# Four of six w_down groups as seven block products, with x kept in memory meanwhile

## The chip, the cores and the metric

The kernel runs on one core of one Trainium2 chip. The metric is the device time of the execution in microseconds (us); the time before is the median of three runs. PE is the tensor engine, DVE the vector engine, ACT the scalar engine, POOL the general engine and SP the engine that issues the DMAs. "Row" in a fence of the instruction order is one instruction as the program lists it for its engine; such a row has no time.

## The reference, cut

A decoder trunk of two layers, float32: a retention layer, a projection of shared keys and values, a dilated-attention layer, each followed by the channel mixer that the change touches. D_MODEL is 1024, SEQ 512, D_FF 2816 (22 tiles of 128).

```
def conv_ffn(h, w_up, conv_w, conv_b, w_down):
    u = h @ w_up                                   # 512 x 5632
    gate, val = u[..., :D_FF], u[..., D_FF:]
    gp = jnp.pad(gate, ((0, 0), (CONV_WIDTH - 1, 0), (0, 0)))
    conv = conv_b
    for i in range(CONV_WIDTH):
        conv = conv + conv_w[i] * gp[:, i:i + S]
    return (jax.nn.gelu(conv, approximate=True) * val) @ w_down
...
f = conv_ffn(rmsnorm(x, norm_ffn_pre[layer]), ...)
x = x + rmsnorm(f, norm_ffn_post[layer])
```

## The kernel before, in words

**Products in two parts.** Each float32 operand is split into a high part (a cast to fp32r, on ACT) and a low part (operand less high part, on DVE). `mm3` (L208 to L210) forms a product as three matmuls: high by high, high by low, low by high. Weights come as units of 128 x 1024 floats: a DMA of 512 KB on SP's queue into a `raw` tile, the cast `whi` (L168, ACT), the low part `wlo` (L169, DVE). Tiles come from pools with a fixed number of buffers (5 each for `whi` and `wlo`), so a cast waits until PE has read the unit that held its buffer. Activations go through `split` (L198 the cast on ACT, L199 the low part on DVE).

**The FFN.** It works on transposed activations. `up(f)` takes two units of `w_up` (gate and value) against the normed h, 8 steps deep: 2 x 8 x 3 = 48 matmuls of 128 x 512 into two accumulators of PSUM (`pm`, tag "mm", 4 buffers). `gated` then makes tile f of the activations: conv on ACT (L553) and DVE (L556, twice), gelu (L559), the product with the value (L561), and the split into `ah` and `al` (8 buffers each).

`contract` multiplies a group of activation tiles by their rows of `w_down`: for each of 4 row blocks b of 128 tokens and 2 column halves c of 512, one PSUM block `po` (tag "po", 2 buffers) of 4 tiles x 3 = 12 matmuls, which `accumulate` adds to the float32 sum `m[b][:, half(c)]` in SBUF (L271 on DVE; for the first group L269, a copy on ACT). The groups are tiles 0 and 1, then 2 to 5, 6 to 9, 10 to 13, 14 to 17, 18 to 21. `up_first` computes tiles 0 and 1; then the ups of a group come, and after them the contraction of the group before it. The last group goes to `finish`, which also does the closing norm, adds to x (L305), and starts the next layer's norm (L254 or L256) and transposes (L264).

**Order.** A tile scheduler places the instructions of each engine in one queue, not always in the order in which they are written; at run time every engine works its queue in order and waits at its head. All weight loads are issued by SP, in order too. In the first FFN of the profiled execution the first matmul of the ups is at 423 us, in the second at 1359 us, and the second FFN runs to the end.

Of the kernel before, what the change touches and what calls it, by code (L numbers as in the profile page):

```python
# [10 lines left out]
F32 = mybir.dt.float32  # L11
F32R = mybir.dt.float32r
# [5 lines left out]
P = 128  # L18
# [57 lines left out]
def _run(gen):  # L76
    for _ in gen:
        pass


def _take(gen, n):
    for _ in range(n):
        next(gen)
# [13 lines left out]
def trunk(ctx: ExitStack, tc: tile.TileContext, a, out):  # L97
# [4 lines left out]
    norm = ctx.enter_context(tc.tile_pool(name="norm", bufs=1))  # L102
    small = ctx.enter_context(tc.tile_pool(name="small", bufs=5))
    ps = ctx.enter_context(tc.tile_pool(name="ps", bufs=2, space=PSUM))

# [159 lines left out]
    def accumulate(src, dst, first):  # L267
        if first:
            nc.scalar.copy(out=dst, in_=src)  # L269
        else:  # L270
            nc.vector.tensor_add(out=dst, in0=src, in1=dst)  # L271

    def contract(left, w, first, tag="po", after=None):


        for b in range(NB):
            for c in range(2):
                po = ps.tile([P, 512], F32, name="po", tag=tag, bufs=4 if tag == "mm" else 2)
                for j in range(len(w)):
                    mm3(po, left(j, b), (w[j][0][:, half(c)], w[j][1][:, half(c)]), j == 0, j == len(w) - 1)  # L280
                    if j < len(w) - 1:
                        yield
                accumulate(po, m[b][:, half(c)], first)
                if after is not None:
                    after(b, c)
                yield

    E = mybir.EngineType
    F4=1
# [251 lines left out]
    def ffn(l, pool, post, then, late, ahead=()):  # L541
        w_up, w_down = a["ffn_w_up"][l], a["ffn_w_down"][l]
        cw = lambda i, f: cols[l][:, i * FT + f : i * FT + f + 1]
        with pool as tmp:

            def up_mm(pm, w, s):
                for k in range(KT):
                    c = slice(k * P, (k + 1) * P)
                    mm3(pm[:, s], (w[0][:, c], w[1][:, c]), (hi[:, k, s], lo[:, k, s]), k == 0, k == KT - 1)

            def gated(f, pg, pv):
                t = tmp.tile([P, SEQ], F32, name="conv", tag="conv", bufs=2)
                nc.scalar.activation(t, pg, AF.Identity, bias=cw(3, f), scale=cw(2, f))  # L553
                for i in (1, 0):
                    d = 2 - i
                    nc.vector.scalar_tensor_tensor(  # L556
                        out=t[:, d:], in0=pg[:, : SEQ - d], scalar=cw(i, f), in1=t[:, d:], op0=ALU.mult, op1=ALU.add
                    )
                nc.scalar.activation(t, t, AF.Gelu_apprx_tanh)  # L559
                act = tmp.tile([P, SEQ], F32, name="act", tag="act", bufs=2)  # L560
                nc.vector.tensor_mul(out=act, in0=t, in1=pv)  # L561
                ah = tmp.tile([P, SEQ], F32R, name="ah", tag="ah", bufs=8)
                al = tmp.tile([P, SEQ], F32R, name="al", tag="al", bufs=8)
                split(act, ah, al)
                return ah, al

            def up(f):
                w = cols_unit(w_up, f * P), cols_unit(w_up, FF + f * P)
                pm = [ps.tile([P, 512], F32, name="pm", tag="mm", bufs=4) for _ in range(2)]
                for g in range(2):  # L570
                    up_mm(pm[g], w[g], slice(0, SEQ))
                return gated(f, *pm)

            def up_first(units, late):

                pm = [ps.tile([P, 512], F32, name="pm", tag="mm", bufs=4) for _ in range(4)]
                with tc.manual_schedule(engines=ORD):
                    for i in range(4):
                        if i == 3:
                            late[1]()  # L580
                        up_mm(pm[i], units[i], slice(0, SEQ // 2))
                        if i == 0:
                            late[0]()
                for i in range(4):
                    up_mm(pm[i], units[i], slice(SEQ // 2, SEQ))
                return [gated(f, pm[2 * f], pm[2 * f + 1]) for f in range(2)]

            def down(fs, act, pool=None):
                w = [unit(w_down[f * P : (f + 1) * P, :], pool=pool if i < 3 else None) for i, f in enumerate(fs)]
                return lambda j, b: [t[:, blk(b)] for t in act[j]], w  # L590

            bounds = [0, *range(2, FT + 1, 4)]
            prev = None
            for n, (f0, f1) in enumerate(zip(bounds, bounds[1:])):
                act = up_first(*late) if n == 0 else [up(f) for f in range(f0, f1)]
                if prev is not None:
                    _run(contract(*down(*prev), n == 1))
                prev = (range(f0, f1), act)
            l, w = down(*prev, tmp)
            return finish(l, w, post, then, ahead, early=tmp)  # L600

# [413 lines left out]
```

## Time and profile before

| | |
|---|---|
| median of three runs | 1729.71 us (1728.86 to 1730.98) |
| profiled execution | 1732.5 us |
| its span | 1730.7 us |
| mean granted clock of PE | 0.995 |
| PE, DVE, ACT, POOL busy | 1703.0, 934.5, 612.1, 396.8 us |
| moved by DMA | 156.10 MB |

The span is what the instructions cover; the execution's own time has 1.8 us more around it. Busy rows name line, engine, operation and "out<-in" by the program's names, then the shape, how many, the busy time, the mean of one in ns, and behind the second bar the idle time ahead of them and what ended it. In a timeline a row gives start and duration in us, and in brackets the idle time ahead and its releaser. In rows of windows each engine's busy time is followed by the number of its instructions, then the granted clock (PEclk, 1.00 is full), the DMA share and GB/s.

### The profile page before, as it was taken

The page shows a single profiled execution, that of the slowest core. Times are in us where ns is not written, and L with a number is a line of the kernel's source. Part 1 is how long each engine was busy: PE and PEld are TensorE (multiplying, and loading weights), DVE is VectorE, ACT ScalarE, POOL GpSimd, SP SyncE. Part 2 cuts the span into 40 slices and gives each one's busy share as a digit, 9 for nine tenths or more (in the row PEclk, how much of TensorE's full clock was granted, in tenths as well). Part 3 has the DMA queues.
Part 4 walks back from the last instruction along what each step waited for, and adds up shares of the span by engine and source line. Part 5 has one row for each costly group of instructions (what it writes and reads, how often), then busy time and mean ns, then how long its engine had stood idle before and what let it go on. Part 6 is the DMA issues. An engine that isn't in the chain of part 4 may idle for free.

```text
span 1730.7 us, 21655 instructions
## 1 busy us (share of the span) xinstructions
PE 1703.0 (98%) x8590; PEld 1412.4 (82%) x8590; DVE 934.5 (54%) x1470; ACT 612.1 (35%) x1070; POOL 396.8 (23%) x281
## 2 busy tenths in 40 slices
PE   9999999999999999998999999999999999999998
PEld 6888888887888888888788888888887888888886
DVE  4563545558544544558556466456474854454454
ACT  5232422325442322324144243244255534233241
POOL 1000000004000000036756656566431300000003
PEclk9999999999999999999999999999999999999999
DMA  6422322213432332331322222222221333333331
GB/s 209 130 67 86 91 97 80 86 49 98 127 97 82 110 98 85 110 109 60 96 74 74 86 74 74 79 76 78 74 74 49 94 106 97 91 102 97 89 107 49
DMA packets 202162, 156.10 MB, mean 90 GB/s; under 512 B 4989, under 2 KB 182093, under 8 KB 202062
## 3 DMA queue, kind: packets, MB, share of 16 engines
q1 hardware_dynamic: 202062, 154.73, 29.2%
q8 instruction: 67, 1.10, 0.3%
q14 instruction: 33, 0.27, 0.0%
HBM read 152.62 MB, written 2.10 MB: 89 GB/s over the span
## 4 chain that ended last, share of the span: by engine, by line
PE 91%; POOL 3%; DVE 3%; DMA 1%; issue 1%; ACT 1%; POOLq 0%; SPq 0%; DVEq 0%; ACTq 0%
PE pm L208 21%; PE pm L210 21%; PE pm L209 21%; PE po L208 6%; PE po L209 6%; PE po L210 6%; PE sc L756 2%; PE po L866 2%; PE pt L846 2%; DVE x L305 1%; PE s L450 1%; POOL r_rms L215 1%; POOL h L323 1%; DVE wlo L169 1%; PE pt L264 1%
## 5 line engine op out<-in xcount | busy, mean ns | idle before, releaser
L208 PE MATMUL pm<-hT_hi,whi 128*128 128x512 f32 (+1 forms) x1424 | 545.0, 383 | 0.0
L209 PE MATMUL pm<-hT_lo,whi 128*128 128x512 f32 (+1 forms) x1424 | 538.4, 378 | 0.8 <-DVE hT_lo L199 0.8
L210 PE MATMUL pm<-hT_hi,wlo 128*128 128x512 f32 (+1 forms) x1424 | 538.9, 378 | 0.0
L169 DVE TENSOR_TENSOR wlo<-raw,whi 128x1024 fp32r<-128x1024 f32 x275 | 371.5, 1356 | 297.0 <-ACT whi L168 293.5
L168 ACT CAST whi<-raw 128x1024 fp32r<-128x1024 f32 x275 | 286.0, 1050 | 641.0 <-PE pm L209 348.9
L208 PEld LDWEIGHTS pm<-hT_hi,whi 128*128 128x128 f32 x1424 | 268.4, 189 | 51.1 <-issue 3.2
L210 PEld LDWEIGHTS pm<-hT_hi,wlo 128*128 128x128 f32 x1424 | 268.2, 188 | 50.3
L209 PEld LDWEIGHTS pm<-hT_lo,whi 128*128 128x128 f32 x1424 | 268.6, 189 | 48.7 <-DVE hT_lo L199 1.7
L158 POOL TENSOR_TENSOR raw<-raw,cols 128x1024 f32<-128x1024 f32 x72 | 145.1, 2017 | 455.2 <-DMA raw<-in_att_w_kv 373.2
L271 DVE TENSOR_TENSOR m<-po,m 128x512 f32<-128x512 f32 x112 | 77.1, 688 | 138.0 <-PE po L210 137.8
L208 PE MATMUL pm<-whi,hT_hi 128*128 128x512 f32 (+1 forms) x384 | 142.1, 370 | 0.0
L208 PE MATMUL po<-whi,ah 128*128 128x512 f32 x352 | 137.1, 390 | 0.0
L209 PE MATMUL po<-wlo,ah 128*128 128x512 f32 x352 | 137.0, 389 | 0.0
L210 PE MATMUL po<-whi,al 128*128 128x512 f32 x352 | 136.9, 389 | 0.0
L210 PE MATMUL pm<-whi,hT_lo 128*128 128x512 f32 (+1 forms) x384 | 136.9, 356 | 0.0
L209 PE MATMUL pm<-wlo,hT_hi 128*128 128x512 f32 (+1 forms) x384 | 136.8, 356 | 0.0
L323 POOL TENSOR_TENSOR h<-m,gain 128x512 f32<-128x512 f32 x28 | 41.9, 1496 | 405.5 <-DVE m L271 405.2
L215 POOL TENSOR_TENSOR r_gn<-v_gn,nhalf 128x1 f32<-128x1 f32 x16 | 8.8, 548 | 357.4 <-DVE v_gn L480 357.4
L208 PEld LDWEIGHTS pm<-whi,hT_hi 128*128 128x128 f32 x384 | 73.0, 190 | 11.6 <-issue 1.0
L209 PEld LDWEIGHTS pm<-wlo,hT_hi 128*128 128x128 f32 x384 | 73.0, 190 | 10.9 <-DVE wlo L169 0.7
L210 PEld LDWEIGHTS pm<-whi,hT_lo 128*128 128x128 f32 x384 | 72.9, 190 | 10.6 <-DVE hT_lo L199 0.2
L208 PEld LDWEIGHTS po<-whi,ah 128*128 128x128 f32 x352 | 66.1, 188 | 14.0 <-DVE m L271 0.4
(137 smaller groups left out, 1958.5 us busy)
## 6 DMA issues: line engine op xcount, KB each, us to landing
raw<-in_ffn_w_up SPq DMA_DIRECT2D x88, 512.0 KB, 3.8
raw<-in_att_w_kv SPq DMA_DIRECT2D x48, 512.0 KB, 4.0
raw<-in_ret_w_in SPq DMA_DIRECT2D x47, 512.0 KB, 3.8
raw<-in_ffn_w_down SPq DMA_DIRECT2D x44, 512.0 KB, 3.2
raw<-in_att_w_q SPq DMA_DIRECT2D x24, 512.0 KB, 3.7
raw<-in_ret_w_out SPq DMA_DIRECT2D x16, 512.0 KB, 3.2
raw<-in_att_w_o SPq DMA_DIRECT2D x8, 512.0 KB, 3.2
x<-in_x SPq DMA_DIRECT2D x3, 512.0 KB, 6.8
```

The costliest lines, as they stand in the source:

```text
L158: nc.gpsimd.tensor_mul(out=dst, in0=dst, in1=gain.unsqueeze(2).broadcast_to(list(src.shape)))
L168: nc.scalar.copy(out=hi, in_=raw)
L169: nc.vector.tensor_sub(out=lo, in0=raw, in1=hi.bitcast(F32))
L208: nc.tensor.matmul(o, lhsT=l[0], rhs=r[0], start=start, stop=False)
L209: nc.tensor.matmul(o, lhsT=l[0], rhs=r[1], start=False, stop=False)
L210: nc.tensor.matmul(o, lhsT=l[1], rhs=r[0], start=False, stop=stop)
L215: behind.append(nc.gpsimd.tensor_tensor(out=r, in0=v, in1=nhalf, op=ALU.pow).ins)
L271: nc.vector.tensor_add(out=dst, in0=src, in1=dst)
L323: eng.tensor_mul(out=mg[b][c], in0=m[b][:, half(c)], in1=gain[:, half(c)])
L756: nc.tensor.matmul(pm[h][:, i, c], lhsT=q, rhs=k, start=True, stop=True)
L846: nc.tensor.transpose(out=pt[:, h, n, :], in_=p[:, h, :], identity=ident)
L866: nc.tensor.matmul(dst, lhsT=v, rhs=p, start=i == 0 and g == 0, stop=i == 7)
```

## The change

For the groups 2 to 5, 6 to 9, 10 to 13 and 14 to 17 of both layers, the product of activations (512 tokens by 512 deep) with rows of `w_down` (512 deep by 1024 columns) is formed by Strassen's scheme, in the variant with shared sums. Tokens are halved (0 to 255, 256 to 511), depth is halved into even and odd tiles of the group, columns into 0 to 511 and 512 to 1023.

- `sums` makes, for each pair of tiles, four sums of activation blocks of 256 columns and splits them: one takes the place of the second half of the even tile's `ah` and `al`, three go to new tiles `sx` (in three buffers of the tag "xwlo").
- `contract7` loads the four weight blocks (128 x 2 x 512 each, in the tags "xraw" and "xwhi"), makes four differences of weights on DVE (L303, L304, L307, L310), splits seven weight operands (`parts`, L170 and L171), and runs the seven products in the order 1, 7, 6, 4, 5, 2, 3. Each has two blocks of 128 tokens (tag "po" with 2 buffers for the first, "mm" with 4 for the second) of 2 x 3 = 6 matmuls, added to the sum of that product over the groups, `q[i]`.
- `q[i]` takes 14 blocks of 128 x 512: eight lie in `m`, six in three tiles that take x's buffers. So x goes to memory (`away`) ahead of the ups and is read back after the combination.
- `combine7` makes the four blocks of the result out of the seven sums, with 14 additions of 128 x 512 (L332), once per layer after the group 14 to 17.
- The order of work becomes: `up_first`, the writes of x, ups 2 to 6, group 2 to 5, ups 7 to 10, group 6 to 9, ups 11 to 14, group 10 to 13, ups 15 to 18, group 14 to 17 with the combination and the reloads of x, ups 19 to 21, the group of tiles 0 and 1, and the last group in `finish`. Matmuls per group fall from 96 to 84.

```
+    away = [dram.tile([P, D], F32, name=f"away{b}") for b in range(NB)]
...
+    def contract7(left, src, first, raws, q):
+        w11, w12, w21, w22 = raws
+        for j, c, t in ((0, 0, w11), (0, 1, w12), (1, 1, w22), (1, 0, w21)):
+            nc.sync.dma_start(out=t.rearrange("p (g n) -> p g n", g=2), in_=src(j, c))
+        w = {}
+        def ready():
+            w[1] = parts(w11)
+            yield
+            nc.vector.tensor_sub(out=w11, in0=w12, in1=w11)
+            nc.vector.tensor_sub(out=w12, in0=w22, in1=w12)
+            w[7] = parts(w12)
+            yield
+            nc.vector.tensor_sub(out=w12, in0=w22, in1=w11)
+            w[6] = parts(w12)
+            yield
+            nc.vector.tensor_sub(out=w12, in0=w21, in1=w12)
+            w[4] = parts(w12)
+            yield
+            for i, t in ((5, w11), (2, w21), (3, w22)):
+                w[i] = parts(t)
+                yield
+        units = ready()
+        _take(units, 4)
+        for i in (1, 7, 6, 4, 5, 2, 3):
+            for r, (tag, n) in enumerate((("po", 2), ("mm", 4))):
+                po = ps.tile([P, 512], F32, name="po", tag=tag, bufs=n)
+                for p in range(2):
+                    mm3(po, left(i, p, r), [t[:, half(p)] for t in w[i]], p == 0, p == 1)
+                accumulate(po, q[i][r], first)
+            next(units, None)
+
+    def combine7(q):
+        for r in range(2):
+            q1, q2, q3, q4, q5, q6, q7 = (q[i][r] for i in range(1, 8))
+            for dst, src in ((q6, q1), (q1, q2), (q5, q6), (q3, q5), (q5, q7), (q4, q6), (q4, q7)):
+                nc.vector.tensor_add(out=dst, in0=dst, in1=src)
...
-                split(act, ah, al)
+                n = slice(0, SEQ // 2 if seven(f) and f % 2 == 0 else SEQ)
+                split(act[:, n], ah[:, n], al[:, n])
+                if seven(f):
+                    pair.append((act, ah, al))
+                    if f % 2:
+                        sums((f - SEVEN[0]) // 2 % 2)
+                        pair.clear()
...
+            SEVEN = 2, 18
+            def sums(p):
...
+                (a0, h0, l0), (a1, _, _) = pair
+                nc.vector.tensor_add(out=u[:, t0], in0=a0[:, t1], in1=a1[:, t1])
+                split(u[:, t0], h0[:, t1], l0[:, t1])
+                nc.vector.tensor_sub(out=u[:, t1], in0=a0[:, t0], in1=a0[:, t1])
+                split(u[:, t1], *dst(1))
+                nc.vector.tensor_sub(out=u[:, t0], in0=u[:, t0], in1=a0[:, t0])
+                split(u[:, t0], *dst(0))
+                nc.vector.tensor_sub(out=u[:, t0], in0=a1[:, t0], in1=u[:, t0])
+                split(u[:, t0], *dst(2))
...
-            bounds = [0, *range(2, FT + 1, 4)]
-            prev = None
-            for n, (f0, f1) in enumerate(zip(bounds, bounds[1:])):
-                act = up_first(*late) if n == 0 else [up(f) for f in range(f0, f1)]
-                if prev is not None:
-                    _run(contract(*down(*prev), n == 1))
-                prev = (range(f0, f1), act)
+            acts = dict(enumerate(up_first(*late)))
+            for b in range(NB):
+                nc.sync.dma_start(out=away[b], in_=x[b])
+            q = {i: [m[r + 2 * h][:, half(c)] for r in range(2)] for i, h, c in ((1, 0, 0), (3, 0, 1), (4, 1, 0), (5, 1, 1))}
+            for b, i in enumerate((2, 6, 7)):
+                t = const.tile([P, D], F32, name=f"q{b}", tag=f"x{b}")
+                q[i] = [t[:, half(r)] for r in range(2)]
+            for f in range(2, FT):
+                acts[f] = up(f)
+                f0 = f - 4
+                if seven(f0) and f0 % 4 == 2:
+                    down7(f0, [acts[f0 + i] for i in range(4)], group[f0], f0 == SEVEN[0], q)
+                    if f == SEVEN[1]:
+                        combine7(q)
+                        for b in range(NB):
+                            x[b] = const.tile([P, D], F32, name=f"x{b}", tag=f"x{b}")
+                            nc.sync.dma_start(out=x[b], in_=away[b])
+                if seven(f) and f % 4 == 1:
+                    group[f - 3] = list(sx)
+            _run(contract(*down(range(2), [acts[0], acts[1]]), False))
+            prev = (range(FT - 4, FT), [acts[f] for f in range(FT - 4, FT)])
```

Lines of the new kernel used below: L171 is the low part of a weight, L273 the addition of a block in `accumulate`, L332 an addition of `combine7`, L710 the reload of x, L157 a weight load; L210 to L212 are `mm3`. "PE_49", "DVE_49", "Activation_49" and names with DMAHW are semaphores of the engine or queue that is waited for.

On DVE before, the end of the group 14 to 17 of the first layer and what follows (the `al` of an up, then the eight additions of the group 14 to 17, then those of the last group in between low parts of the next stage):

```order
L169 TENSOR_TENSOR wlo_5636<-raw_5634,whi_5637 128x1024 [waits DMAHW2_49,Activation_49]
L199 TENSOR_TENSOR al_5477<-act_5474,ah_5476 128x512 [waits Activation_49]
L271 TENSOR_TENSOR m0_77<-po_5504,m0_77 128x512 [waits PE_49]
L271 TENSOR_TENSOR m0_77<-po_5518,m0_77 128x512 [waits PE_49]
L271 TENSOR_TENSOR m1_78<-po_5532,m1_78 128x512 [waits PE_49]
```

And on DVE after, the end of the group 14 to 17 of the first layer, whose last two blocks are added here, among the combination's additions; `wlo_5538` and `wlo_5544` belong to up 19, `wlo_5611` to up 20:

```order
L332 TENSOR_TENSOR m0_83<-m0_83,q0_3546 128x512 [waits DVE_49]
L273 TENSOR_TENSOR m0_83<-po_5498,m0_83 128x512 [waits PE_49]
L332 TENSOR_TENSOR m1_84<-m1_84,q0_3546 128x512 [waits DVE_49]
L332 TENSOR_TENSOR m0_83<-m0_83,m2_85 128x512 [waits DVE_49]
L273 TENSOR_TENSOR m1_84<-po_5506,m1_84 128x512 [waits PE_49]
L332 TENSOR_TENSOR m2_85<-m2_85,q2_3548 128x512 [waits DVE_49]
L332 TENSOR_TENSOR m1_84<-m1_84,m3_86 128x512 [waits DVE_49]
L332 TENSOR_TENSOR m3_86<-m3_86,q2_3548 128x512
L332 TENSOR_TENSOR m3_86<-m3_86,q2_3548 128x512 [waits DVE_49]
L171 TENSOR_TENSOR wlo_5538<-raw_5536,whi_5539 128x1024 [waits DMAHW3_49,Activation_49]
L171 TENSOR_TENSOR wlo_5544<-raw_5542,whi_5545 128x1024 [waits DMAHW4_49,Activation_49]
L171 TENSOR_TENSOR wlo_5611<-raw_5609,whi_5612 128x1024 [waits DMAHW5_49,Activation_49]
```

Before, the low parts of the next stage's weights stood ahead of the group's additions; now those of the next up stand behind all additions of the group and of the combination.

On PE after, at the same place, the last matmuls of the group's seventh product (`po_5506`) and the first ones of up 19 (`pm_5548`, `pm_5549`) and up 20 (`pm_5621`):

```order
L212 MATMUL po_5506<-whi_5447,sx_5116 128x512
L210 MATMUL pm_5548<-hT_hi_87,whi_5539 128x512 [waits Activation_49]
L211 MATMUL pm_5548<-hT_lo_88,whi_5539 128x512
L210 MATMUL pm_5549<-hT_hi_87,whi_5545 128x512 [waits DVE_49,Activation_49]
L211 MATMUL pm_5549<-hT_lo_88,whi_5545 128x512
L210 MATMUL pm_5621<-hT_hi_87,whi_5612 128x512 [waits DVE_49,Activation_49]
L211 MATMUL pm_5621<-hT_lo_88,whi_5612 128x512
L212 MATMUL pm_5548<-hT_hi_87,wlo_5538 128x512 [waits DVE_49]
L210 MATMUL pm_5548<-hT_hi_87,whi_5539 128x512
```

Six matmuls that need only high parts were pulled ahead; the seventh takes the low part that stands last on DVE.

On SP after, the issues around the reloads (`raw_5615` is the second unit of up 20, `raw_5755` and what follows belong to the last contractions):

```order
L157 DMA raw_5609<-in_ffn_w_up 128x8x128 [waits DMAHW5_49,DMAHW2_49,DVE_49]
L157 DMA raw_5868<-in_att_w_kv 128x4x256 [waits DVE_49]
L710 DMA x1_5530<-away1_73 128x1024 [waits DVE_49]
L710 DMA x0_5528<-away0_72 128x1024 [waits DVE_49]
L710 DMA x2_5532<-away2_74 128x1024 [waits DVE_49]
L157 DMA raw_5615<-in_ffn_w_up 128x8x128 [waits DMAHW3_49,DVE_49]
L157 DMA raw_5682<-in_ffn_w_up 128x8x128 [waits DMAHW4_49,DVE_49]
```

Three reloads of x now stand ahead of the second unit of up 20 and of both units of up 21.

More of the change, by code (lines that the diff above doesn't have):

```diff
@@ L104, in trunk @@
     ps = ctx.enter_context(tc.tile_pool(name="ps", bufs=2, space=PSUM))
+    dram = ctx.enter_context(tc.tile_pool(name="dram", bufs=1, space=bass.MemoryType.DRAM))
+    away = [dram.tile([P, D], F32, name=f"away{b}") for b in range(NB)]
     nhalf = const.tile([P, 1], F32, name="nhalf")
@@ new lines, in ffn @@
+            SEVEN = 2, 18
+            seven = lambda f: SEVEN[0] <= f < SEVEN[1]
+            pair, sx, group = [], [], {}
+            def sums(p):
+                if p == 0:
+                    sx[:] = [
+                        tmp.tile([P, D], F32R, name="sx", tag="xwlo", bufs=3).rearrange("p (s n) -> p s n", s=4)
+                        for _ in range(3)
+                    ]
+                (a0, h0, l0), (a1, _, _) = pair
+                t0, t1 = slice(0, SEQ // 2), slice(SEQ // 2, SEQ)
+                u = norm.tile([P, 512], F32, name="h", tag="h", bufs=HB)
+                dst = lambda j: (sx[j][:, p, :], sx[j][:, 2 + p, :])
+                nc.vector.tensor_add(out=u[:, t0], in0=a0[:, t1], in1=a1[:, t1])
[6 more added lines that the diff above has]
+                split(u[:, t0], *dst(2))
@@ new lines, in down7, with left, src @@
+            def down7(f0, act, sums_, first, q):
+                def left(i, p, r):
+                    rows = slice(r * P, (r + 1) * P)
+                    late_rows = slice(SEQ // 2 + r * P, SEQ // 2 + (r + 1) * P)
+                    even, odd = act[2 * p], act[2 * p + 1]
+                    if i in (1, 2):
+                        return [t[:, rows] for t in (even if i == 1 else odd)]
+                    if i in (4, 5):
+                        return [t[:, late_rows] for t in (odd if i == 4 else even)]
+                    t = sums_[{6: 0, 7: 1, 3: 2}[i]]
+                    return t[:, p, rows], t[:, 2 + p, rows]
+                def src(j, c):
+                    w = w_down[f0 * P : (f0 + 4) * P, half(c)]
+                    return w.rearrange("(g j p) n -> j p g n", g=2, j=2)[j]
+                raws = [
+                    tmp.tile([P, D], F32, name="raw", tag=tag, bufs=n)
+                    for tag, n in (("xraw", 1), ("xwhi", 3), ("xwhi", 3), ("xwhi", 3))
+                ]
+                contract7(left, src, first, raws, q)
```

## The prediction

> **What bounds the kernel now.** I read the busy shares first, then the chain that ended last, then what the tensor engine waits for.
>
> ```profile
> span 1730.7 us, 21655 instructions
> PE 1703.0 (98%) x8590; PEld 1412.4 (82%) x8590; DVE 934.5 (54%) x1470; ACT 612.1 (35%) x1070; POOL 396.8 (23%) x281
> PE 91%; POOL 3%; DVE 3%; DMA 1%; issue 1%; ACT 1%; POOLq 0%; SPq 0%; DVEq 0%; ACTq 0%
> ```
> ```profile
> engine line waited for: us in total, times, longest us
> PE pt L264 <- DVE h L256: 7.9, 8, 2.0
> PE pt L264 <- DVE h L254: 4.8, 3, 3.0
> ```
>
> PE is busy for 98% of the span and carries 91% of the chain. Its two largest waits come to 7.9 and 4.8 us, both at transposes where a norm ends, outside the groups that change. So every matmul taken away shortens the kernel by its issue interval, as long as nothing else makes PE wait. Windows inside the first FFN say how much room the others have:
>
> ```profile
> core 0: us, PE busy (x) PEld busy (x) DVE busy (x) ACT busy (x) POOL busy (x), PEclk, DMA share, GB/s
> 500.00:600.00 100.00, 100.00 (x443) 82.81 (x442) 45.44 (x53) 33.82 (x42) 0.00 (x0) 1.00 0.31 95
> 600.00:700.00 100.00, 100.00 (x443) 82.81 (x442) 44.37 (x54) 27.64 (x34) 0.00 (x0) 1.00 0.28 85
> ```
>
> PE never stops there; DVE works 45 us in 100, ACT 28 to 34, and the transfers take 0.3 of the DMA time.
>
> **Term 1: matmuls removed.** The busy time of a matmul overlaps the next one's, so I take the interval between starts:
>
> ```profile
> 399.95 0.40 PE L210 MATMUL po<-whi,hT_lo 128*128 128x512 f32 x1
> ...
> 408.12 0.39 PE L210 MATMUL po<-whi,hT_lo 128*128 128x512 f32 x1
> ```
>
> 36 matmuls lie between the two starts: 8.17 / 36 = 0.227 us. (The windows agree: 100 / 443 = 0.226.) A group of four tiles has 8 blocks of 12 matmuls, 96 in all; as seven products it has 7 x 2 row halves x 2 tiles deep x 3 = 84. Twelve fewer, four groups, two layers: 96 matmuls x 0.227 = **-21.8 us**. The two tiles left over (0 and 1) keep their 48 matmuls, only later.
>
> **Term 2: inside the seven products.** One now lasts 84 x 0.227 = 19.0 us on PE, 2.72 us a product. What DVE and ACT must do beside it has these prices (mean ns after the bar, from 470 to 550 us):
>
> ```profile
> L169 DVE TENSOR_TENSOR wlo<-raw,whi 128x1024 fp32r<-128x1024 f32 x15 | 18.4, 1225 | 30.8 <-ACT whi L168 30.1
> L168 ACT CAST whi<-raw 128x1024 fp32r<-128x1024 f32 x15 | 15.8, 1055 | 29.1 <-PE pm L209 29.1
> L556 DVE SCALAR_TENSOR_TENSOR conv<-pm,cols,conv 128x510 f32<-128x510 f32 (+1 forms) x13 | 9.7, 746 | 0.2
> L561 DVE TENSOR_TENSOR act<-conv,pm 128x512 f32<-128x512 f32 x7 | 4.8, 688 | 13.9 <-PE pm L210 13.9
> L269 ACT COPY m<-po 128x512 f32<-128x512 f32 x8 | 4.7, 587 | 4.7 <-PE po L210 4.7
> L199 DVE TENSOR_TENSOR al<-act,ah 128x512 fp32r<-128x512 f32 x6 | 4.1, 683 | 0.0
> ```
> ```profile
> L199 DVE TENSOR_TENSOR sl<-t,sh 128x256 fp32r<-128x256 f32 x4 | 1.7, 425 | 1.9 <-ACT sh L198 1.9
> ```
>
> Over one period (four ups and one group) DVE did 4 x (2 x 0.75 + 0.69 + 0.68 + 2 x 1.22) = 21 us for the ups, plus 4 x 1.22 + 8 x 0.69 = 10 for the group. It now does seven low parts (8.6), four weight differences of the same size (4.9), 14 accumulates (9.7), and per pair of tiles four adds and four splits of 256 columns less half a split (about 8 x 0.42 - 0.26 = 3.1, twice): 21 + 29 = 51 us in 4 x 10.9 + 19.0 = 63 us. That is 80%, where 45% stood; PE keeps its place as the bound on average. Locally it is tighter. Inside the 19 us stand 14 accumulates and seven low parts, 8.6 + 9.7 = 18.3 us by busy times, three of its own weights and four of the next ups', which now stand between accumulates. A low part there waits for its cast, whose buffer PE frees one product after another; the accumulates behind it then run late by cast and low part, 1.06 + 1.22 = 2.3 us at most, beginning from when PE frees it. PE feels this only when a product finds its accumulator block unread: each tag of blocks holds a block until the second next product, 2 x 2.72 less the half product that fills it, 4.08 us. So I take 0. No row shows DVE this full beside PE; the low end is 0 (nothing here can be faster than the matmuls), the high end is rival 2. In the first group ACT copies instead (14 x 0.587 + 7 x 1.055 = 15.6 us of 19.0): 0 as well. The sums of products end during the up that stands between the last tile and the group, 10.9 us of cover.
>
> **Term 3: the end of the last group, once per layer.** The 14 combining adds and the last ten accumulates stand in DVE's queue ahead of the low part for the next up. Before, that place looked like this, on DVE:
>
> ```profile
> 549.06 1.22 DVE L169 TENSOR_TENSOR wlo<-raw,whi 128x1024 fp32r<-128x1024 f32 x1
> 550.20 0.68 DVE L199 TENSOR_TENSOR al<-act,ah 128x512 fp32r<-128x512 f32 x1
> 550.92 0.69 DVE L271 TENSOR_TENSOR m<-po,m 128x512 f32<-128x512 f32 x1
> 553.64 0.69 DVE L271 TENSOR_TENSOR m<-po,m 128x512 f32<-128x512 f32 x1 [2.03 <-PE po L210]
> ...
> 567.24 0.69 DVE L271 TENSOR_TENSOR m<-po,m 128x512 f32<-128x512 f32 x1 [2.03 <-PE po L210]
> 569.00 1.23 DVE L169 TENSOR_TENSOR wlo<-raw,whi 128x1024 fp32r<-128x1024 f32 x1 [1.07 <-ACT whi L168]
> 570.15 0.68 DVE L271 TENSOR_TENSOR m<-po,m 128x512 f32<-128x512 f32 x1
> 570.75 2.35 DVE L169 TENSOR_TENSOR wlo<-raw,whi 128x1024 fp32r<-128x1024 f32 x2
> ```
>
> DVE waited 2.03 us for each of the later blocks, and the low parts for the next up were started in those gaps. A 512-wide add next to an independent one costs 0.60 (570.15 to 570.75); one by itself lasts 0.69. Now a block comes every 1.36 us, and between two blocks stand an accumulate and a combining add, 1.2 to 1.4 us: the gaps are full. With 0 at the first matmul of the group: the last weight set's buffer is freed after the second product at 5.44, so its low part ends near 5.44 + 1.06 + 1.22, some 7.9 with what stands ahead of it; the next 10 accumulates and 10 adds take 12.0 (at 0.60) to 13.8 us (at 0.69), so 19.9 to 21.7, where PE is done at 19.04. Four more adds: 22.3 to 24.4. The low part: 23.4 to 25.6. PE has six matmuls that need no low part (two for each of three accumulators), till 19.04 + 6 x 0.227 = 20.4, and then waits 3.0 to 5.2 us. Most of these adds depend on the one ahead, which speaks for the 0.69 end: I take 4.2, twice: **+8.4 us**. What is late next: the low parts of the other three weight units follow at 1.2 us each, while PE has 22 matmuls (5 us) per accumulator; they are in time.
>
> **Term 4: the clock after that stall.** The rows of before show three idle times of this size:
>
> ```profile
> 411.22 0.66 PE L264 MATMUL pt<-ident,h 128*128 128x128 f32 x4 [2.03 <-DVE h L256]
> 412.99 0.63 PE L210 MATMUL po<-whi,hT_lo 128*128 128x512 f32 x1
> 413.41 0.63 PE L208 MATMUL po<-whi,hT_hi 128*128 128x512 f32 x1
> ```
> ```profile
> 412.00:416.00 4.00, 4.00 (x14) 3.26 (x14) 3.98 (x5) 3.04 (x8) 2.21 (x3) 0.57 0.00 0
> 1348.00:1352.00 4.00, 4.00 (x14) 3.21 (x13) 3.42 (x4) 2.51 (x7) 2.43 (x3) 0.64 0.00 0
> ```
> ```profile
> 782.78 1.09 PE L264 MATMUL pt<-ident,h 128*128 128x128 f32 x8 [2.96 <-DVE h L254]
> 784.00:788.00 4.00, 4.00 (x19) 3.31 (x18) 4.00 (x5) 2.61 (x8) 1.70 (x3) 1.00 0.00 0
> ```
>
> The first ends at 411.22; the granted clock in the next window is 0.57 and the matmuls come 0.42 us apart (412.99 to 413.41). The window after 1348 shows 0.64 in the same place of the other layer. After 2.96 us at 782.78 the clock stayed 1.00. A low window costs 4.0 x (1 - 0.57) = 1.7 us. Low end 0, high end 2.0 a stall; I take 1.8, since two of three dropped: **+3.6 us**. The Trainium skill ("TensorE: Matmul & The Clock Gate", The HAM clock gate) has the clock halve only after an idle window of about 3.4 us that runs freely; by it a stall near 4 us may or may not cover a window, and the term would lie between 0 and half of 3.4 us a stall. The trace agrees about the half clock and about the chance in it, and does not agree that 3.4 us of idleness are needed: 2.03 were enough.
>
> **Term 5: x to memory and back, eight 512 KB transfers per layer and the loads queued behind them.**
>
> ```profile
> raw<-in_ffn_w_up SPq DMA_DIRECT2D x88, 512.0 KB, 3.8
> x<-in_x SPq DMA_DIRECT2D x3, 512.0 KB, 6.8
> ```
>
> The reloads wait for the last reads of the tiles that held sums (up to 24.4), and one weight load of the next up stands behind the third on SP. It is issued near 24.4 and lands after 3.8 to 6.8, its cast and low part are done by 31 to 34; PE, restarted at 24.6 with 66 matmuls ahead of it, needs it at 39.6. The writes stand before the ups' loads early in the FFN, where the DMA share is 0.3. x itself is wanted only at the end of the layer, more than 30 us on. I take 0; the high end is rival 3.
>
> **Sum.** -21.8 + 0 + 8.4 + 3.6 + 0 = -9.8 us. The profiled execution took 1732.5 (span 1730.7 and 1.8 around it), 2.8 above the median of the runs, 1729.7; it would become 1722.7, and the median **1720 us**. By the ends of terms 3 and 4 alone: -21.8 + 6.0 + 0 to -21.8 + 10.4 + 4.0, or 1714 to 1722.
>
> **Rivals.** (1) *No stall at the combine*: the adds fit between the blocks. For it: 0.60-spaced adds leave 0.16 us of slack in every 1.36. Against: even then four adds and a low part, 3.6 us, stand after the last block, and PE has 1.4 us of work. It gives 1729.7 - 21.8 = 1708. Chance 0.10.
> (2) *DVE becomes the bound inside the seven products* and the result is slower. Its place is every group: low parts that wait for casts hold the accumulates back by more than 4.08 us, and a product stands still. For it: 18.3 us of DVE work in 19.0. Against: the 2.3 us that I find. Eight groups share it, so above 1.7 us each, 8 x 1.7 - 9.8 = +3.8, it is slower than before; at 3 us each the time is 1720 + 24 = 1744. Chance 0.12.
> (3) *The reloads hold the up's weights*: four transfers one after the other at 3.8 to 6.8 us would land the unit at 24.4 + 15 to 27, done by 42 to 54 against 39.6, 2 to 14 us twice. Against: at share 0.31 the DMA moved 95 GB/s, so 512 KB take about 1.7 us of all engines. With 4 us twice: 1728, about no change. Chance 0.11.
> (4) *The clock stays full* after the stall, as after 782.78: 1720 - 3.6 = 1716. This is the case that the skill's clock-gate section makes for a stall which covers no whole window. Chance 0.17.
>
> **How the numbers follow.** The forecast has 0.50. With 0.2% (3.5 us) as what can be told from no change: (1), (4), the forecast and the short end of (3) are faster, 0.80; the rest of (3) is the same, 0.08; (2) is slower, 0.12. The range goes from (1) at 1708 to the long end of (3) near 1731; it leaves out (2) and little else. The likeliest case alone has 1714 to 1723.
>
> **What would show it.** Right: 96 matmuls fewer; PE at 100% through the seven products of each of the first three groups; once per layer a PE idle of 3 to 5 us released by a low part on DVE, a few matmuls after the last product; behind it a window of low clock; outside the FFNs the same times. Wrong: PE idle inside the groups, released by an accumulate (rival 2); idle about 20 us after the combine, released by a cast or a transfer (rival 3); no idle there (rival 1).

## The result, and the profile after

The changed kernel takes 1720.36 us (median of six runs, 1718.13 to 1722.74) against 1729.95 before (six runs): a ratio of 0.9946, 95% interval 0.9933 to 0.9958. It is faster by 9.6 us where 9.8 were forecast. The profiled execution took 1719.35 us, 13.2 less than that of before; why the two differences differ is told below.

The page of the changed kernel begins:

```profile
span 1717.5 us, 21852 instructions
PE 1682.1 (98%) x8494; PEld 1394.2 (81%) x8494; DVE 1083.7 (63%) x1718; ACT 661.9 (39%) x1170; POOL 389.8 (23%) x281
```

96 matmuls fewer, and 149 us more of DVE's work. What PE waited for:

```profile
engine line waited for: us in total, times, longest us
PE pt L266 <- DVE h L258: 8.8, 8, 2.3
PE pm L212 <- DVE wlo L171: 6.8, 2, 3.4
PE pt L266 <- DVE h L256: 3.9, 2, 3.0
```

One row is new: PE waits twice, 3.4 us each, for the low part of a weight. The others are the norms' transposes, as before. Inside the groups PE does not wait, as a period of one group and four ups shows:

```profile
566.00:628.60 62.60, 62.60 (x278) 51.81 (x277) 47.41 (x66) 25.58 (x36) 0.00 (x0) 1.00 0.33 101
```

DVE is busy for 47.4 of 62.6 us there. The new wait is at the end of the last group. PE in the first FFN:

```profile
709.50 0.39 PE L212 MATMUL po<-whi,sx 128*128 128x512 f32 x1
709.73 0.39 PE L210 MATMUL pm<-hT_hi,whi 128*128 128x512 f32 x1
...
710.86 0.39 PE L211 MATMUL pm<-hT_lo,whi 128*128 128x512 f32 x1
714.66 0.70 PE L212 MATMUL pm<-hT_hi,wlo 128*128 128x512 f32 x1 [3.41 <-DVE wlo L171]
715.16 0.63 PE L210 MATMUL pm<-hT_hi,whi 128*128 128x512 f32 x1
...
718.15 0.42 PE L211 MATMUL pm<-hT_lo,whi 128*128 128x512 f32 x1
718.41 0.39 PE L212 MATMUL pm<-hT_hi,wlo 128*128 128x512 f32 x1
```

The six matmuls without a low part, the wait, then nine matmuls in the 3.75 us from 714.66 to 718.41 instead of 9 x 0.227 = 2.04: 1.7 us lost to the clock. The windows show the grant:

```profile
712.00:716.00 4.00, 1.34 (x3) 1.07 (x4) 4.00 (x6) 0.00 (x0) 0.00 (x0) 0.85 0.49 160
716.00:720.00 4.00, 4.00 (x14) 3.18 (x13) 0.88 (x1) 0.22 (x1) 0.00 (x0) 0.72 0.85 246
```

In the second FFN the wait ends at 1643.59, and seven matmuls take 3.10 us instead of 1.59:

```profile
1643.59 0.79 PE L212 MATMUL pm<-hT_hi,wlo 128*128 128x512 f32 x1 [3.40 <-DVE wlo L171]
...
1646.69 0.40 PE L210 MATMUL pm<-hT_hi,whi 128*128 128x512 f32 x1
```

And DVE at the same place of the first FFN; PE's first matmul of the group is 19.04 us ahead of 709.73, at 690.69:

```profile
697.42 1.23 DVE L171 TENSOR_TENSOR wlo<-raw,whi 128x1024 fp32r<-128x1024 f32 x1 [0.29 <-ACT whi L170]
698.56 1.28 DVE L273 TENSOR_TENSOR q<-po,q 128x512 f32<-128x512 f32 x2
...
702.82 0.68 DVE L332 TENSOR_TENSOR m<-m,q 128x512 f32<-128x512 f32 x1
703.42 0.69 DVE L273 TENSOR_TENSOR m<-po,m 128x512 f32<-128x512 f32 x1
704.02 0.68 DVE L332 TENSOR_TENSOR m<-m,q 128x512 f32<-128x512 f32 x1
...
707.21 0.69 DVE L273 TENSOR_TENSOR q<-po,q 128x512 f32<-128x512 f32 x1
...
708.57 0.69 DVE L273 TENSOR_TENSOR m<-po,m 128x512 f32<-128x512 f32 x1
...
710.38 0.68 DVE L273 TENSOR_TENSOR m<-po,m 128x512 f32<-128x512 f32 x1
...
712.18 1.28 DVE L332 TENSOR_TENSOR m<-m,q 128x512 f32<-128x512 f32 x2
713.39 3.49 DVE L171 TENSOR_TENSOR wlo<-raw,whi 128x1024 fp32r<-128x1024 f32 x3
720.87 1.23 DVE L171 TENSOR_TENSOR wlo<-raw,whi 128x1024 fp32r<-128x1024 f32 x1 [3.99 <-ACT whi L170]
```

From 697.42 to the three low parts at 713.39 DVE has no gap of more than 0.1 us. The accumulates at 707.21 and 708.57 stand 1.36 us apart, the pace at which PE finishes blocks: by then DVE had caught up with PE. The last accumulate starts at 710.38, four adds follow, and only then the low part that PE has wanted since 711.1.

**Splitting a time into work and clock.** Every run has a span and a mean granted clock. Span x clock is what the span would be at full clock; the rest is clock lost. One run's clock is known to 0.001, 1.7 us, so I take means over all runs of a kernel (its runs of before are those beside it on the same chip; for the changed kernel, which has no such clocks of before, those of the first experiments; at full clock before stood at 1720.7 to 1721.1 us in every set). One execution of the kernel before, of 6053.64 us, is left out. In every kept trace (one profiled execution of each kernel) the clock is also low for the last microseconds of the span, behind PE's last matmul, where it costs PE nothing: 1.5 to 3.1 us of each lost clock are of this kind (2.2 before, 3.0 in the changed kernel), and the times at full clock are too low by as much. So a difference of 1 us between two rows of that column says little.

| kernel | runs | median us | ratio to before (95%) | at full clock, us | lost clock, us |
|---|---|---|---|---|---|
| before, beside the first four experiments | 14 | 1730.92 | 1 | 1720.7 | 8.4 |
| changed | 6 | 1720.36 | 0.9946 (0.9933 to 0.9958) | 1705.9 | 12.6 |
| before, 96 matmuls left out | 4 | 1708.75 | 0.9874 (0.9859 to 0.9890) | 1699.7 | 7.3 |
| combine left out | 4 | 1708.54 | 0.9872 (0.9858 to 0.9886) | 1700.4 | 6.4 |
| combine later | 4 | 1712.62 | 0.9896 (0.9882 to 0.9910) | 1700.7 | 10.3 |
| two groups | 11 | 1732.09 | 1.0004 (0.9995 to 1.0013) | 1716.4 | 13.4 |
| stall filled | 5 | 1718.80 | 0.9927 (0.9914 to 0.9939) | 1706.9 | 10.0 |
| no transfers of x | 5 | 1719.00 | 0.9930 (0.9917 to 0.9942) | 1705.3 | 11.7 |
| low parts twice | 4 | 1720.86 | 0.9940 (0.9926 to 0.9953) | 1705.7 | 13.3 |
| low parts three times | 4 | 1775.35 | 1.0254 (1.0238 to 1.0269) | 1752.0 | 22.2 |
| combine on POOL | 5 | 1715.19 | 0.9919 (0.9905 to 0.9932) | 1703.4 | 9.6 |
| combine later, norms filled | 4 | 1714.70 | 0.9915 (0.9901 to 0.9928) | 1708.0 | 4.7 |
| before, norms filled | 9 | 1733.45 | 1.0021 (1.0012 to 1.0031) | 1726.8 | 4.8 |
| combine later, norms filled briefly | 4 | 1708.78 | 0.9875 (0.9859 to 0.9892) | 1702.0 | 5.1 |

At full clock the change took away 1720.7 - 1705.9 = 14.8 us. Terms 1 and 3 with the measured waits give -21.8 + 2 x 3.4 = -15.0.

The kept traces can be compared without this column. In them the clock is either full or half, and half clock comes in stretches of 3.41 us, so one stretch beside busy matmuls costs 1.7 us. Ahead of PE's last matmul the kernel before has four such stretches, the changed one five: 1730.7 - 4 x 1.7 = 1723.9 and 1717.5 - 5 x 1.7 = 1709.0, 14.9 apart.

### The profile page after: what moved, and what is told of

The parts are those of the page before. It is cut to its first block, busy times and chain, and to the rows that moved or that the text cites. A ratio compares the mean times of both kernels' runs of the same rounds, so it can differ in the third digit from the quotient of the medians.

```text
span 1717.5 us, 21852 instructions
## 1 busy us (share of the span) xinstructions
PE 1682.1 (98%) x8494; PEld 1394.2 (81%) x8494; DVE 1083.7 (63%) x1718; ACT 661.9 (39%) x1170; POOL 389.8 (23%) x281
## 5 line engine op out<-in xcount | busy, mean ns | idle before, releaser
L171 DVE TENSOR_TENSOR wlo<-raw,whi 128x1024 fp32r<-128x1024 f32 x299 | 405.1, 1359 | 223.7 <-ACT whi L170 222.3
L212 PE MATMUL pm<-hT_hi,wlo 128*128 128x512 f32 (+1 forms) x1424 | 539.3, 379 | 6.8 <-DVE wlo L171 6.8
L210 PE MATMUL pm<-hT_hi,whi 128*128 128x512 f32 (+1 forms) x1424 | 545.8, 383 | 0.0
L170 ACT CAST whi<-raw 128x1024 fp32r<-128x1024 f32 x299 | 313.0, 1051 | 530.7 <-PE pm L211 255.4
L212 PEld LDWEIGHTS pm<-hT_hi,wlo 128*128 128x128 f32 x1424 | 268.6, 189 | 58.1 <-DVE wlo L171 7.7
L210 PEld LDWEIGHTS pm<-hT_hi,whi 128*128 128x128 f32 x1424 | 269.0, 189 | 51.2 <-issue 3.2
L160 POOL TENSOR_TENSOR raw<-raw,cols 128x1024 f32<-128x1024 f32 x72 | 139.7, 1941 | 448.1 <-DMA raw<-in_att_w_kv 374.1
L210 PE MATMUL pm<-whi,hT_hi 128*128 128x512 f32 (+1 forms) x384 | 141.9, 369 | 0.0
L212 PE MATMUL pm<-whi,hT_lo 128*128 128x512 f32 (+1 forms) x384 | 136.7, 356 | 0.0
L273 DVE TENSOR_TENSOR m<-po,m 128x512 f32<-128x512 f32 x112 | 75.3, 685 | 45.3 <-PE po L212 45.0
L211 PE MATMUL po<-wlo,ah 128*128 128x512 f32 x224 | 87.8, 392 | 0.0
L210 PE MATMUL po<-whi,ah 128*128 128x512 f32 x224 | 87.8, 392 | 0.0
L212 PE MATMUL po<-whi,al 128*128 128x512 f32 x224 | 87.6, 391 | 0.0
L210 PEld LDWEIGHTS pm<-whi,hT_hi 128*128 128x128 f32 x384 | 72.9, 190 | 11.5 <-issue 1.0
L212 PEld LDWEIGHTS pm<-whi,hT_lo 128*128 128x128 f32 x384 | 72.8, 190 | 10.6 <-DVE hT_lo L201 0.2
L602 DVE SCALAR_TENSOR_TENSOR conv<-pm,cols,conv 128x511 f32<-128x511 f32 x88 | 65.6, 746 | 6.6 <-ACT conv L599 5.4
```

Source lines behind the costliest of these rows:

```text
L160: nc.gpsimd.tensor_mul(out=dst, in0=dst, in1=gain.unsqueeze(2).broadcast_to(list(src.shape)))
L170: nc.scalar.copy(out=hi, in_=raw)
L171: nc.vector.tensor_sub(out=lo, in0=raw, in1=hi.bitcast(F32))
L210: nc.tensor.matmul(o, lhsT=l[0], rhs=r[0], start=start, stop=False)
L211: nc.tensor.matmul(o, lhsT=l[0], rhs=r[1], start=False, stop=False)
L212: nc.tensor.matmul(o, lhsT=l[1], rhs=r[0], start=False, stop=stop)
```

## The experiments

**What the matmuls are worth, alone.** The kernel before, with the last of the eight blocks left out in the four groups of both layers:

```
-                    _run(contract(*down(*prev), n == 1))
+                    _run(contract(*down(*prev), n == 1, blocks=8 if n == 1 else 7))
```

> The kernel before, with the last of the 8 blocks (12 matmuls and its accumulate) left out in the groups 2 to 5, 6 to 9, 10 to 13 and 14 to 17 of both layers: 96 matmuls fewer, and none of the change's other work. Theory (0.227 us a matmul, nothing else on the path): 21.8 us less than before, 1708 us (1706.5 to 1709.5). Rival (other engines take up part of it): 1712 us or more.

1708.75 us, 22.2 less than before (1708.75 against 1730.92; by the interval 19 to 24), and 21.0 less at full clock. The price of 0.227 us a matmul holds; the rival's 1712 us or more lies outside the interval, but a part of 1 us that goes to other engines is not excluded.

**The combining adds behind up 19.**

```
-                    if f == SEVEN[1]:
-                        combine7(q)
+                if f == SEVEN[1] + 1:
+                    combine7(q)
```
(the four reloads of x stand under the same `if` and move with the adds)

> The 14 combining adds and the reloads of x are written after up 19 instead of ahead of it, so that the two low parts of up 19 stand on DVE between the group's last accumulates; nothing else moves. Theory (the price of the change is the wait at the combine, 3.4 us, and the lower clock behind it, 1.5 to 1.7 us, once per layer): both go, 10 us less than the changed kernel, 1710 us (1708 to 1712), no PE wait on a low part left. Rival (what the matmuls should have brought is lost inside the groups or to the transfers of x): unchanged at 1720 us.

1712.62 us, just above the range that the theory gave. The waits on a low part are gone from the list of PE's waits. On DVE both low parts of up 19 now stand between accumulates of the group:

```profile
701.14 1.22 DVE L171 TENSOR_TENSOR wlo<-raw,whi 128x1024 fp32r<-128x1024 f32 x1
702.27 0.68 DVE L273 TENSOR_TENSOR m<-po,m 128x512 f32<-128x512 f32 x1
702.98 1.22 DVE L171 TENSOR_TENSOR wlo<-raw,whi 128x1024 fp32r<-128x1024 f32 x1
```

At full clock the kernel needs 1700.7 us, 5.2 less than the changed one, for 6.8 us of waits taken away. The kept traces settle the rest: both kernels have five stretches of half clock there, and their spans, 1717.5 and 1710.7, are 6.8 us apart. The order of DVE is the cause of the stall; that it is the adds and not the reloads is shown by the next experiment, which leaves the reloads where the change has them.

**No combining adds at all.**

```
-                        combine7(q)
```

> The 14 combining adds are left out in both layers (the sums of the seven products stay uncombined), the reloads of x stay. Theory (only the adds' place on DVE makes PE wait): as with the adds moved, 1710 us within 1.5 us. Rival (the adds cost time wherever they stand, 14 x 0.6 = 8.4 us of DVE a layer): some 3 to 8 us less than the kernel with the adds moved.

1708.54 us, 4.1 less than with the adds moved; theory said the same within 1.5, and the rival 3 to 8 less. But at full clock the two are equal (1700.4 and 1700.7): 3.9 of the 4.1 us are clock. The kept traces agree: 1707.0 with three stretches of half clock is 1701.9 without them, and 1710.7 with five is 1702.2. Windows over the end of the attention layer, where no part of the change works, of the kernel with the adds moved:

```profile
1330.00:1352.00 22.00, 19.60 (x95) 15.98 (x94) 20.12 (x23) 12.09 (x29) 13.85 (x16) 0.92 0.42 155
```

and of the one without them:

```profile
1330.00:1352.00 22.00, 18.96 (x108) 15.51 (x107) 21.03 (x24) 12.56 (x29) 14.04 (x17) 1.00 0.42 150
```

22 x 0.08 = 1.8 us lie between the two at a norm whose instructions are the same. The rival's numbers fit the median; its reason (adds that cost wherever they stand) does not fit the waits or the full-clock times.

**Two groups instead of four.**

```
-            SEVEN = 2, 18
+            SEVEN = 2, 10
```
(and the groups 10 to 13 and 14 to 17 through `contract`)

> Only the groups 2 to 5 and 6 to 9 are seven products; 10 to 13 and 14 to 17 are contracted with 96 matmuls as in the kernel before; combine and reloads follow the second group. Theory (12 x 0.227 = 2.7 us won per group, 5 us lost once per layer): -10.9 + 10 = -1 us, 1729 us (1727 to 1731). Rival (the loss belongs to every group, so it halves with the gain): half of the gain, 1725 us.

1732.09 us, no change from before (0.9995 to 1.0013), 1 us above the theory's range and far from the rival's. At full clock it is 4.3 us less than before: -10.9 + 6.8 = -4.1, with PE's waits on a low part at 6.8 us in two as in the full change. The lost clock is 5.0 us more, where I had put 3.2. The gain goes with the groups and the loss with the layers: two groups pay for one combination, and no more.

**The stall filled.** Twelve matmuls that nobody reads stand between the last product and up 19:

```
+                        fill = ps.tile([P, 512], F32, name="fill", tag="po", bufs=2)
+                        for k in range(12):
+                            nc.tensor.matmul(fill, lhsT=hi[:, k % KT, 0:P], rhs=hi[:, k % KT, :], start=k == 0, stop=k == 11)
                         combine7(q)
```

> The changed kernel with 12 idle matmuls (into a block that nobody reads, 12 x 0.227 = 2.7 us) between the last product of the last group and up 19, where PE waits 3.4 us. Nothing is taken off DVE, so the low part comes at the same time. Theory (after an idle time of this size the granted clock is halved for 3 to 4 us, which costs 1.5 to 1.7 us): the wait shrinks to about 0.7 us, no window behind it is below 0.95, and the time falls by 3 us to 1717 (1716 to 1718.5). Rival 1 (the clock does not follow from that idle time): 1720 us. Rival 2 (the matmuls are simply added): 1725 us.

PE of this kernel, and its window over the place:

```profile
711.11 2.88 PE L709 MATMUL fill<-hT_hi 128*128 128x512 f32 x12
...
716.04 0.50 PE L212 MATMUL pm<-hT_hi,wlo 128*128 128x512 f32 x1 [0.69 <-DVE wlo L171]
716.37 0.39 PE L210 MATMUL pm<-hT_hi,whi 128*128 128x512 f32 x1
```
```profile
700.00:760.00 60.00, 59.31 (x261) 48.66 (x260) 42.59 (x57) 21.65 (x25) 7.89 (x4) 1.00 0.43 132
```

The wait is 0.69 us and the matmul behind it is followed after 0.33, the next after 0.23: full clock. The same place of the second FFN has no low clock either. The 24 matmuls more per program cost at most about 1 us (1706.9 at full clock against 1705.9). The time is 1718.8, just above the theory's range and within rival 1's reach by its distance alone; against before it is 0.9927, the changed kernel 0.9946, so 3.3 us, but the two intervals overlap. The lost clock fell by 2.6 us; in the kept trace the two stretches of half clock behind the stalls are gone. That the time fell rests on these rows more than on the median.

**No transfers of x.** x is not kept; three tiles go on from zeros that POOL writes.

> The changed kernel without the eight transfers of x per layer: x is not kept, and goes on from zeros that POOL writes into three tiles after the combine. Theory (the transfers are hidden; the load behind the reloads lands in time): 1720 us within 1.5. Rival (the reloads hold weight loads back, or compete with them): faster by 2 us or more.

1719.0 us, inside the theory's range. The ratio is 2.8 us below that of the changed kernel, with overlapping intervals, and at full clock the two are 0.6 us apart (1705.3 and 1705.9). I see no cost of the transfers; that there is none of 2 or 3 us rests on the full-clock times alone.

**Low parts twice, and three times.** How near DVE is to being the bound, with the low parts of a group's seven weights written more than once:

```
-        nc.vector.tensor_sub(out=lo, in0=raw, in1=hi.bitcast(F32))
+        for _ in range(times):
+            nc.vector.tensor_sub(out=lo, in0=raw, in1=hi.bitcast(F32))
```

> The changed kernel with each low part of the seven weights of a group written twice: 7 x 1.15 = 8 us more of DVE's time per group, 59 of 63 us in the period. Theory (DVE has about 12 us to spare per group, and an accumulate may come 4.08 us late): PE waits little, 1720 to 1728 us. Rival (the group is at its limit now): each of the eight groups loses a good part of the 8 us, 1745 us or more.

> The same with each of these low parts written three times: 16 us more per group, 67 us of DVE in a period of 63. Both theories: DVE is the bound from here, some 4 to 5 us per group and more for its order, 1755 us or above; how far the time lies from that shows the room that there was.

Twice: 1720.86 us, 0.9940, the same as the changed kernel. The period then looks like this:

```profile
566.00:628.60 62.60, 62.60 (x278) 51.87 (x277) 54.92 (x73) 25.88 (x35) 0.00 (x0) 1.00 0.34 101
```

DVE at 54.9 of 62.6 us, 88%, and PE never stops. Three times: 1775.35, 55 us more than the changed kernel, 20 above what I had set as the lower bound. Its list of PE's waits:

```profile
PE pm L213 <- DVE wlo L172: 23.8, 6, 9.6
PE po L212 <- DVE wlo L172: 15.9, 20, 1.8
PE po L211 <- DVE q L274: 2.2, 8, 0.4
```

PE now waits for low parts inside the groups (20 times) and at their ends (6 times, up to 9.6 us), and hardly for accumulates. It is the low parts that this kernel makes longer, so it does not tell what PE would wait for if DVE were filled with other work. 46 us are full-clock time, 10 are lost clock.

**The adds on POOL.**

```
-                nc.vector.tensor_add(out=dst, in0=dst, in1=src)
+                nc.gpsimd.tensor_add(out=dst, in0=dst, in1=src)
```

> The changed kernel with the 14 combining adds on POOL, at their place in the program. Theory (POOL is idle there, an add of 512 columns takes about 1.5 us on it, 21 us a layer, and the sums are wanted 33 us later): no PE wait on a low part, 1711 to 1714 us, as with the adds moved on DVE. Rival (DVE gets slower while POOL adds, and the accumulates behind it come late): 1716 us or more.

1715.19 us, between the two theories. The waits for low parts of 3.4 us are gone, but a new one has come 34 us later in the first FFN, in the group of tiles 0 and 1. PE:

```profile
748.45 0.80 PE L210 MATMUL po<-whi,ah 128*128 128x512 f32 x1 [3.34 <-DVE m L273]
```

ACT and, while POOL adds (700 to 722 us), the low parts on DVE:

```profile
743.06 1.05 ACT L170 CAST whi<-raw 128x1024 fp32r<-128x1024 f32 x1 [3.25 <-POOL raw L160]
744.01 0.77 ACT L599 ACTIVATE conv<-pm,cols 128x512 f32<-128x512 f32 x1
```
```profile
L171 DVE TENSOR_TENSOR wlo<-raw,whi 128x1024 fp32r<-128x1024 f32 x6 | 9.9, 1643 | 7.8 <-ACT whi L170 7.8
```

A cast for the next layer stands at the head of ACT's queue and waits for a scaling on POOL; behind it the conv of up 21, behind that on DVE its two steps, the gating and then the accumulate that PE waits for. POOL itself had no work then; it had waited 18 us for a load:

```profile
741.13 1.90 POOL L160 TENSOR_TENSOR raw<-raw,cols 128x1024 f32<-128x1024 f32 x1 [18.02 <-DMA raw<-in_att_w_kv]
```

SP issued that load at 735.80, where the kernel with the adds moved on DVE has it at 733.09. Ahead of it on SP stand the reloads of x, and the last of them left only at 723.13, when POOL was done with the adds (712.25 to 716.18 with the adds moved). So the adds, slower on POOL, probably held the loads back through the reloads, which is rival 3's path; no run takes the two apart. The low parts took 1.64 us on average beside POOL's adds instead of 1.22.

**The clock at the norms.** Idle matmuls ahead of the first block's transposes, first 12 in each norm, with the adds moved and in the kernel before:

```
+        if b == 0:
+            fill = ps.tile([P, 512], F32, name="fill", tag="tr")
+            for k in range(12):
+                nc.tensor.matmul(fill[:, 0:P], lhsT=ident, rhs=ident, start=k == 0, stop=k == 11)
```

> The kernel with the combining adds moved behind up 19, and 12 idle matmuls of 128 x 128 (1.8 us) ahead of the first block's transposes in each norm, where PE waits 2.0 to 3.0 us for a normed row on DVE. They are in PE's queue right ahead of the transposes. Theory (what still separates this kernel from 21.8 us less than before is clock lost after those waits, up to 1.7 us each at three places, which no part of the change touches): 3 to 5 us less than with the moved adds alone, 1708 to 1710 us. Rival (the remainder belongs to the change): 1712 to 1713 us, or later by what the matmuls take.

> The kernel before with the same 12 idle matmuls at the same places, as a control without any part of the change. Theory: 2 to 5 us less than before, 1726 to 1729 us, the windows after these waits at a clock of 1.00. Rival (idle times of 2 us don't set the clock): 1730 to 1732 us.

Both misses: 1714.70, and 1733.45, slower than before (1.0012 to 1.0031). The filling was too long. In the kernel before with it, PE shows

```profile
410.84 2.84 PE L264 MATMUL fill<-ident 128*128 128x128 f32 x24
```

24 instructions for 12 matmuls and some 2.7 us where I had taken 1.8 from the transposes and the wait was 2.03. The lost clock did fall (10.3 to 4.7 us with the adds moved, 6.9 to 4.8 before, against the runs beside it), but the full-clock time rose by 7.3 and 5.7. With half as many and none at the start of the kernel:

> The kernel with the adds moved behind up 19, with 6 idle matmuls (2.72 / 2 = 1.4 us by the run with 12, which took 2.72 us and were longer than the wait that they were to fill) ahead of the first block's transposes of each later norm, not at the kernel's start. Theory (the moved adds leave only clock that is lost after the norms' waits, 10 us in this kernel against 6 without the adds): the 2.0 us waits shrink below 1 us, the full-clock part of the time stays, and the time falls to 1707 to 1710 us. Rival (waits below 1 us still cost clock, or the matmuls come late): 1712 to 1714 us.

```profile
409.62 1.50 PE L268 MATMUL fill<-ident 128*128 128x128 f32 x12
411.82 1.39 PE L272 MATMUL pt<-ident,h 128*128 128x128 f32 x8 [0.70 <-DVE h L260]
```

1708.78 us (0.9859 to 0.9892): 21.0 us less than the kernel before beside it, the fastest complete kernel here. Lost clock 5.1 us, full-clock time 1.3 above that of the moved adds alone. How much of the 21.0 belongs to the change is not shown: the shorter filling was not run in the kernel before, whose lost clock the longer one lowered too. The kernel with the moved adds stood 18.3 us under before; of the 3.5 that are left to 21.8, the table puts 1.9 down to lost clock and the rest to the time at full clock; by the kept traces without their stretches of half clock (1723.9 and 1702.2) none of it belongs to the change.

## Why the prediction was right, step by step

**Term 1, -21.8 us.** Right: 22.2 measured alone, 21.0 at full clock.

**Term 2, 0 us.** Right, and with more room than I gave it: DVE works 76% of a period where I had counted 80%, and 88% still costs nothing. Rival 2, that DVE becomes the bound, has its point between 88% and the third writing. Whether late accumulates would then stop PE, as I described it, stays open: in the run with three writings PE mostly waits for the low parts themselves.

**Term 3, +8.4 us.** The place, the releaser and the order were right; the size was 6.8. From the group's first matmul at 690.69, the last weight's low part ended at 7.9, as worked out; the last accumulate began at 19.7 and ended near 20.3 (19.9 to 21.7 worked out), and PE went on at 24.0 (23.4 to 25.6). The failed step is "most of these adds depend on the one ahead, which speaks for the 0.69 end". The rows at 702.82, 703.42 and 704.02 start 0.60 apart, and so do the two adds at 712.18 (1.28 us for both). In the order of the queue they do not depend on the one directly ahead, though they name the same tile: by the program product 1 lies in the first half of `m0` and product 3 in the second, so the add into `m0` and the accumulate of `po_5498` behind it touch different blocks, and the last two adds go into the two halves of `m3`. So the near end, 3.0, was the right one. The other 0.4 us are waits for PE: the ten accumulates and ten adds took 12.4 us from 698.56 to 710.98 instead of 12.0. And since DVE had caught up with PE at 707.21, the adds between the blocks cost little; the wait is made of what stands behind the last block, four adds and a low part, as the answer to rival 1 had it.

**Term 4, +3.6 us.** 1.7 + 1.5 = 3.2 in the profile, and gone when the wait was cut to 0.69 us. The kept traces also show which waits are followed by a low clock. The stretches of half clock last 3.41 us or a multiple of it, and those of one trace begin whole multiples of 3.41 us apart, so the clock changes on a grid of that step. Cut on its grid, the kernel before has at the norm ahead of the first FFN

```profile
408.78:412.19 3.41, 1.38 (x10) 0.88 (x9) 2.77 (x3) 0.28 (x1) 3.18 (x4) 1.00 0.51 154
412.19:415.61 3.42, 3.42 (x12) 2.74 (x11) 3.42 (x5) 2.85 (x8) 1.72 (x2) 0.50 0.00 0
```

and the changed kernel, at the same norm and at the first stall,

```profile
407.60:411.01 3.41, 1.59 (x8) 0.97 (x6) 2.56 (x2) 0.79 (x3) 3.07 (x4) 1.00 0.77 269
411.01:414.43 3.42, 3.21 (x18) 2.77 (x19) 3.42 (x5) 2.41 (x6) 2.84 (x3) 1.00 0.16 47
711.37:714.79 3.42, 0.13 (x1) 0.13 (x2) 3.42 (x6) 0.00 (x0) 0.00 (x0) 1.00 0.43 152
714.79:718.20 3.41, 3.41 (x9) 2.63 (x10) 2.09 (x2) 0.00 (x0) 0.00 (x0) 0.50 0.86 273
```

Before, the whole wait of 2.03 us fell into one step, PE was busy for 1.38 of 3.41 us, and half clock followed; in the changed kernel the same wait fell across two steps, 1.59 in the first, and none followed. Over the 14 kept traces, up to PE's last matmul, all 42 steps at full clock in which PE was busy for at most 0.41 of the time were followed by half clock, two of the seven with 0.43 to 0.47, and none with more. On the Trainium skill's rule ("TensorE: Matmul & The Clock Gate", The HAM clock gate), that it takes an idle window of about 3.4 us: the traces agree with the 3.4 us, but the window need not be idle throughout, since 2.03 us of idleness within it were enough.

**Term 5, 0 us.** Right as far as it can be told. The last three loads behind the reloads left SP from 714.63 on:

```profile
707.17 6.65 SPq L710 DMA_DIRECT2D x<-away  x3
714.63 3.13 SPq L157 DMA_DIRECT2D raw<-in_ffn_w_up  x3
```

and the low part of the first of them began at 720.87, 30.2 after the group's start, against 39.6 when PE wants it. Rival 3 did not come.

**The sum.** By the profiled executions it was -13.2, not -9.8. -21.8 for the matmuls, 6.8 for the two waits, 3.2 for the clock behind them and -1.7, because elsewhere the changed kernel has three stretches of half clock where the old one has four, give -13.5. Such losses differ from execution to execution, which is the spread of the runs; over all runs the changed kernel loses 4.2 us more clock than before, the two stalls' 3.2 and 1.0 besides. So the agreement of the median with the forecast to within 1 us is partly luck: a stall sized 1.6 us too long stood against clock lost elsewhere. Rival 1's -21.8 us is what moving the adds brings once the stretches of half clock are taken off both kept traces: 1723.9 before, 1702.2 with the adds moved.

## What to carry to other kernels

Where one engine is busy for 98% of the span, price an edit in that engine's issue intervals, and then read the other engines' order at the ends of the edit: here 31% of the gain at full clock went into one place per layer where work that nobody needed soon stood ahead of a weight that was needed at once. Moving such work behind the next stage's first operands returned the loss, at no cost that the runs show. A fixed loss per layer also sets how small an edit still pays: with two groups a layer the same change brings nothing.

## What the runs showed of the hardware that I had not expected

- On DVE an operation that takes the result of the one directly ahead starts later than an independent one: in the changed kernel the second conv step starts 0.78 us behind the first (1.53 us for the two at 654.82, 0.75 for the second); with the adds moved, an independent low part starts 0.66 us behind the same step (716.89 to 717.55). The combining adds, whose order keeps such pairs apart, start 0.60 us apart.
- The granted clock changes on a grid of 3.41 us and falls to half for one step or more after a step in which PE was busy for 0.41 of the time or less. So a wait of 2.03 us costs 1.7 us or nothing, by where it falls on the grid. With waits of 0.7 to 0.8 us at two of the three norms, the fastest kernel lost 5 us of clock in all instead of 10.
- A low part of 1024 columns on DVE takes 1.22 us alone. Of six beside POOL's adds three took 1.56 to 2.33 us; the other three took 1.21 to 1.23, and then the add beside them took 2.2 to 2.4 us instead of 1.29. One of the two waits for the other.
- A float32 128 x 128 matmul shows as two instructions and takes 0.22 us, about as long as a 512-wide one of the other kind (0.227).
